# Gate and up stage of a streaming encoder step: row pieces handed out between products, nine row buffers, one preparation moved later

## The chip, the cores and the metric

The kernel runs on one core of a Trainium2 chip. The metric is the device time of one execution in microseconds (us). The core has five engines, each with its own instruction list that it works through in order: TensorE (PE, matmuls, with the weight loads shown as PEld), VectorE (DVE), ScalarE (ACT), GpSimd (POOL) and SyncE (SP, which here only issues DMA transfers). They wait for one another through semaphores.

## What is computed

One layer of a hybrid encoder runs on 2048 prompt rows and 128 sample rows of width 1024: a mixer of banded attention and convolution, a cross-attention into 256 memory tokens, and a dense SwiGLU network with 2816 hidden channels. The change lies in the first half of that network:

```python
D_MODEL = 1024; D_FF = 2816
h = rmsnorm(x, g_ffn_pre)
f = (jax.nn.silu(h @ w_gate) * (h @ w_up)) @ w_down
x = x + rmsnorm(f, g_ffn_post)
```

Everything is float32. The kernel splits each operand of a matmul into a rounded part ("hi", type fp32r) and the rest ("lo") and makes three matmuls of one product: hi by hi, hi by lo and lo by hi.

## The kernel before

The stages run one after the other: memory keys and values, projection, attention, mixer output, cross-attention (`phase_cross`), gate and up (`gate_up`), down. The change touches the end of `phase_cross` and the whole of `gate_up`.

**Cross-attention.** Sixteen tiles of 128 rows pass through scores, softmax (`z`), transposed probabilities (`probs`) and values. Behind some tiles stands `natural(g, p)`. It reads a pair of finished row tiles back (two DMA loads, L1304), norms each (ACT Square L1307, POOL L1309 and L1310, a DVE multiply L1311 over 1024 columns), makes four differences on POOL (L1312 to L1318) and stores seven combinations of the halves to the DRAM buffer `hn[g]` with four DMAs that POOL issues (L1313, L1315, L1317, L1319). There are nine such pairs, three for each of three row groups. A pair is taken as soon as its tiles are done and t is at least 4; the pair of tiles 12 and 14 was taken behind tile 15, and the last pair (13 and 15) in the first double block of `gate_up`.

**Gate and up.** The two matrix products are made with seven products of half size in place of eight (a Winograd-like scheme). For each of three row groups the seven forms of the rows are needed in transposed form: `tform(g, j)` makes one form in three *pieces*. A piece is a row load of 128 x 512 from `hn` (L1392, issued by SP into a buffer `nat`), four PE transposes into a PSUM buffer `tr` (L1395), the ACT copy of hi (L1397) and the DVE subtraction that gives lo (L1398). 21 pieces make a group ready. There were three `nat` buffers and there are two `tr` buffers. For each of 22 weight blocks, `wforms(f)` loads two weight tiles (L1404, L1405, into four buffers `wf`), makes the mixed forms on POOL (L1412 to L1415) and splits all seven (ACT L1417, DVE L1418). Nine buffer pairs `wh`, `wl` hold the split forms, so that two forms of the next block are ready ahead of a product. `product(ps, j, ...)` is 12 matmuls of 384 columns (three for each of four chunks; L283, L284 and L285 are the three matmuls of `mm3`), and a block has seven products. DVE and ACT combine the results (L1454 to L1482), and POOL makes the forms that the down stage reads (L1507 to L1510).

The first group's 21 pieces form *the opening* of the stage; the pieces for the next group are made during the last block of the group before (*the turn*), since each transposed form has one buffer only.

**What sets the order.** A scheduler takes the program's instructions and lays out each engine's list by a simulated clock, with priorities (`high_priority`) and with ties such as `issue_after(x)`, which keeps an instruction from being laid out ahead of x. So the lists differ from the order of the code, and they are fixed before the run. An engine that meets an instruction whose inputs aren't there waits, and all behind it wait too. That holds for SP as well: a row load that waits for its buffer holds up every weight load behind it.

## Time and profile before

| | us |
|---|---|
| median of 3 runs | 2948.85 (2946.77 to 2949.27) |
| the profiled execution | 2949.61 |
| its span in the profile | 2947.8 |
| PE busy | 2872.6 (97% of the span) |
| DVE busy | 2079.8 (71%) |
| POOL busy | 1371.4 (47%) |
| ACT busy | 1308.1 (44%) |

The table says that PE is busy nearly all the time, and that DVE, the next, has a quarter of its time free. These are means over stages that differ. The gate and up stage lies from about 1522 us to about 2490 us of the span; its opening runs from 1522 us to 1564 us, the first turn from about 1850 us to 1910 us, the second from about 2190 us to 2224 us.

### The profile page before, as it was taken

The page shows a single profiled execution, that of the slowest core. Times are in us where ns is not written, and L with a number is a line of the kernel's source. Part 1 is how long each engine was busy: PE and PEld are TensorE (multiplying, and loading weights), DVE is VectorE, ACT ScalarE, POOL GpSimd, SP SyncE. Part 2 cuts the span into 40 slices and gives each one's busy share as a digit, 9 for nine tenths or more (in the row PEclk, how much of TensorE's full clock was granted, in tenths as well). Part 3 has the DMA queues.
Part 4 walks back from the last instruction along what each step waited for, and adds up shares of the span by engine and source line. Part 5 has one row for each costly group of instructions (what it writes and reads, how often), then busy time and mean ns, then how long its engine had stood idle before and what let it go on. Part 6 is the DMA issues. An engine that isn't in the chain of part 4 may idle for free.

```text
span 2947.8 us, 45388 instructions
## 1 busy us (share of the span) xinstructions
PE 2872.6 (97%) x16740; PEld 2624.6 (89%) x16740; DVE 2079.8 (71%) x3024; ACT 1308.1 (44%) x2661; POOL 1371.4 (47%) x1247
## 2 busy tenths in 40 slices
PE   8999999979989999999999999999999999999998
PEld 8999999969978777888879999999999999888786
DVE  6697795969985336344469787788889997555655
ACT  4535364659874234232344333433344444333433
POOL 0268396730022224244557565465556775424413
PEclk9999999989999999999999999999999999999999
DMA  8735255558845665133355333644344446657754
GB/s 303 251 115 174 98 161 171 159 181 199 205 137 189 204 246 172 52 128 109 125 199 184 115 133 115 198 155 154 144 140 151 143 142 231 223 171 226 227 191 163
DMA packets 198474, 500.04 MB, mean 170 GB/s; under 512 B 18981, under 2 KB 87085, under 8 KB 189923
## 3 DMA queue, kind: packets, MB, share of 16 engines
q1 hardware_dynamic: 187931, 461.09, 48.4%
q0 software_dynamic: 10320, 36.05, 3.2%
q8 instruction: 131, 2.15, 0.3%
q14 instruction: 92, 0.75, 0.1%
HBM read 365.97 MB, written 141.81 MB: 172 GB/s over the span
## 4 chain that ended last, share of the span: by engine, by line
PE 43%; DMA 3%; POOL 2%; DVE 2%; issue 1%; ACT 0%; DVEq 0%; SPq 0%; POOLq 0%; ACTq 0%
PE psb L285 14%; PE psb L284 14%; PE psb L283 14%; PE psb L291 1%; DMA sbf<-in_w_down_dram 1%; DMA sbf<-x 1%; POOL sbf L1540 1%; PE psb L1395 1%; DMA sbf<-hn 1%; DVE sbr L1601 0%; POOL sbf L340 0%; DMA hn<-sbf 0%; DMA sbf<-in_w_gate_dram 0%; DVE flexb L1480 0%; DVE sbr L1418 0%
## 5 line engine op out<-in xcount | busy, mean ns | idle before, releaser
L283 PE MATMUL psb<-sbr 128*128 128x384 f32 (+3 forms) x2808 | 943.0, 337 | 3.7 <-ACT sbr L1600 1.5
L284 PE MATMUL psb<-sbr 128*128 128x384 f32 (+3 forms) x2356 | 806.1, 342 | 2.5 <-DVE sbr L320 2.4
L285 PE MATMUL psb<-sbr 128*128 128x512 f32 (+3 forms) x1848 | 633.9, 345 | 1.9 <-DVE sbr L1601 1.8
L283 PEld LDWEIGHTS psb<-sbr 128*128 128x128 f32 x2808 | 530.6, 189 | 33.6 <-ACT sbr L1600 2.6
L285 PE MATMUL psb<-sbr,sbx 128*128 128x384 f32 (+2 forms) x1484 | 476.7, 322 | 0.0
L284 PEld LDWEIGHTS psb<-sbr 128*128 128x128 f32 x2356 | 445.3, 189 | 29.5 <-DVE sbr L320 2.7
L285 PEld LDWEIGHTS psb<-sbr 128*128 128x128 f32 x1848 | 348.5, 189 | 31.4 <-DVE sbr L1601 4.6
L1418 DVE TENSOR_TENSOR sbr<-sbf,sbr 128x512 fp32r<-128x512 f32 x258 | 264.7, 1029 | 36.1 <-ACT sbr L1417 35.3
L1417 ACT CAST sbr<-sbf 128x512 fp32r<-128x512 f32 x258 | 159.4, 620 | 279.2 <-PE psb L284 231.4
L285 PEld LDWEIGHTS psb<-sbr,sbx 128*128 128x128 f32 x1484 | 280.5, 189 | 0.2
L523 DVE SCALAR_TENSOR_TENSOR psb<-sbf,psb 128x768 f32<-128x768 f32 (+1 forms) x290 | 264.2, 911 | 6.2
L291 PE MATMUL psb<-sbr 128*128 128x512 f32 x1004 | 247.3, 395 | 0.1
L1601 DVE TENSOR_TENSOR sbr<-sbf,sbr 128x384 fp32r<-128x384 f32 (+1 forms) x231 | 161.3, 721 | 94.3 <-ACT sbr L1600 93.4
L291 PEld LDWEIGHTS psb<-sbr 128*128 128x128 f32 x1004 | 185.8, 188 | 41.5 <-issue 2.5
L278 POOL TENSOR_TENSOR sbx<-sbf,sbr 128x1024 fp32r<-128x1024 f32 x60 | 152.9, 2550 | 81.2 <-ACT sbr L277 76.1
L1540 POOL TENSOR_TENSOR sbf<-sbf 128x512 f32<-128x512 f32 x77 | 106.2, 1385 | 169.2 <-DMA sbf<-in_w_down_dram 167.6
L1600 ACT CAST sbr<-sbf 128x384 fp32r<-128x384 f32 (+1 forms) x231 | 110.6, 497 | 165.2 <-PE psb L284 137.3
L533 POOL TENSOR_TENSOR flexb<-flexb,flexb 128x128 f32<-128x128 f32 (+1 forms) x180 | 167.4, 931 | 22.4 <-ACT flexb L532 12.9
L283 PE MATMUL psb<-sbr,sbx 128*128 128x384 f32 (+1 forms) x524 | 170.5, 327 | 1.2 <-ACT sbr L1397 0.7
L1417 ACT CAST sbx<-sbf 128x512 fp32r<-128x512 f32 x153 | 94.5, 620 | 160.9 <-PE psb L284 148.9
L291 PE MATMUL psb<-sbr,sbx 128*128 128x512 f32 x654 | 160.7, 397 | 4.1 <-ACT sbx L319 2.2
L1418 DVE TENSOR_TENSOR sbx<-sbf,sbx 128x512 fp32r<-128x512 f32 x153 | 152.4, 998 | 15.3 <-ACT sbx L1417 15.0
(328 smaller groups left out, 5938.8 us busy)
## 6 DMA issues: line engine op xcount, KB each, us to landing
af<-flexb SPq DMA_DIRECT2D x33, 1344.0 KB, 6.0
sbf<-in_w_down_dram SPq DMA_DIRECT2D x154, 256.0 KB, 3.7
sbf<-af SPq DMA_DIRECT2D x90, 384.0 KB, 4.2
sbf<-in_w_gate_dram SPq DMA_DIRECT2D x66, 512.0 KB, 3.3
sbf<-in_w_up_dram SPq DMA_DIRECT2D x66, 512.0 KB, 3.4
sbf<-x SPq DMA_DIRECT2D x50, 512.0 KB, 3.8
sbf<-in_w_in_dram SPq DMA_DIRECT2D x48, 512.0 KB, 3.9
sbr<-ks SPq DMA_DIRECT2D x28, 512.0 KB, 9.6
```

What stands on the lines that cost most here:

```text
L278: self.lo_engine.tensor_tensor(lo[:, :], wf[:, :], hi[:, :].bitcast(F32), ALU.subtract)
L283: nc.tensor.matmul(ps, lh, rh, start=start, stop=False, **kw)
L284: nc.tensor.matmul(ps, lh, rl, start=False, stop=False, **kw)
L285: self.last_product = nc.tensor.matmul(ps, ll, rh, start=False, stop=stop, **kw)
L291: self.last_half = nc.tensor.matmul(y[o], l, r[:, o * 512:(o + 1) * 512], start=start and x == 0, stop=stop and x == 2)
L523: nc.vector.scalar_tensor_tensor(acc if w < CW - 1 else o, src(w), cwt[:, j, w:w + 1], acc, ALU.mult, ALU.add)
L533: nc.gpsimd.tensor_tensor(o, o, v, ALU.add)
L1417: nc.scalar.copy(hs[j][:, :], src[j])
L1418: nc.vector.tensor_tensor(ls[j][:, :], src[j], hs[j][:, :].bitcast(F32), ALU.subtract)
L1540: nc.gpsimd.tensor_tensor(acc[:, :], acc[:, :], q[:, :], ALU.add if s > 0 else ALU.subtract)
L1600: nc.scalar.copy(ch[:, m], a[:, x, m])
L1601: nc.vector.tensor_tensor(cl[:, m], a[:, x, m], ch[:, m].bitcast(F32), ALU.subtract)
```

## The change

Four things change.

1. `nat` gets nine buffers in place of three: six more lie in the region that `natural` uses for its own tiles (offsets 0 to 12).
2. `tform` no longer does the work; it returns the two form tiles and a list of pieces. `next_rows(9)` keeps up to nine row loads out ahead, and `next_piece` does one piece. In `product`, a piece is done after every second chunk (six matmuls), and it is tied with `issue_after` to the last matmul emitted. In the turn the pieces so spread over the last block of a group and the following one.
3. The opening no longer makes whole forms; it takes the 21 pieces one after the other, with nine row loads ahead.
4. In `phase_cross` a pair is prepared only while t is below 15, so the pair of tiles 12 and 14 moves into `gate_up`, where `natural` is called in the first double block for it, and in the second for the pair of tiles 13 and 15.

No instruction is added or removed: each engine's list has as many instructions of each kind as before.

```diff
@@ phase_cross
-                if ready and t >= 4:
+                if ready and 4 <= t < NPT - 1:
@@ gate_up
-                .at("s", 2, (sbF, [26, 28, 38.5])).at("nat", 2, (sbF, [40.5, 42.5, 44.5]))
+                .at("s", 2, (sbF, [26, 28, 38.5])).at("nat", 2, (sbF, [40.5, 42.5, 44.5, 0, 2, 4, 6, 8, 10]))
...
         def tform(g, j):
             hi = self.t(pool, [P, 4, 3 * P], F32R, f"t{j}h")
             lo = self.t(pool, [P, 4, 3 * P], F32R, f"t{j}l")
-            for p in range(3):
+
+            def rows(p):
                 n = PAIRS[g][p][2]
                 x = self.t(pool, [P, 512], F32, "nat")
                 nc.sync.dma_start(x[:n, :], self.hn[g][:n, p, TFORM[j], :])
+                return x
+
+            def piece(p, x):
+                n = PAIRS[g][p][2]
                 ps = self.t(ps_tr, [P, 4, P], F32, "tr")
...
-            return hi, lo
+            return (hi, lo), [(lambda p=p: rows(p), lambda x, p=p: piece(p, x)) for p in range(3)]
+
+        raw, waiting = [], []
+
+        def next_rows(most):
+            while waiting and len(raw) < most:
+                first, second = waiting.pop(0)
+                raw.append((second, first()))
+
+        def next_piece(pin=False):
+            if not raw:
+                return
+            with ExitStack() as stack:
+                if pin:
+                    stack.enter_context(self.tc.issue_after(self.last_product.ins))
+                second, x = raw.pop(0)
+                second(x)
+            next_rows(9)
...
-        def product(ps, j, n, w, start):
+        def product(ps, j, n, w, start, turn=False):
...
+                if k % 2 and not (turn and j == 0):
+                    next_piece(True)
...
             for j in range(7):
-                ts[j] = tform(0, j)
+                ts[j], pieces = tform(0, j)
+                waiting += pieces
+            next_rows(9)
+            while raw:
+                next_piece()
...
-                    def after(j):
-                        if turn:
-                            nxt.append(tform(g + 1, j))
+                    if turn:
+                        for j in range(7):
+                            t, pieces = tform(g + 1, j)
+                            nxt.append(t)
+                            waiting.extend(pieces)
+                        next_rows(9)
...
-                    product(a, 0, n, w, True)
+                    product(a, 0, n, w, True, turn)
...
-                    after(0)
```

(The calls of `after(1)` to `after(6)` go too.) Some lines move by this: the transposes are L1395 before and L1400 after, the DVE subtraction of a piece L1398 and L1403, the row load L1392 and L1393, the weight loads L1404, L1405 and L1426, L1427, the DVE split of a weight form L1418 and L1440.

The first place is PE's list in the opening, at the twelfth and thirteenth pieces; `ident_73` is the identity matrix, `sbf` and `sbr` are the large SBUF tiles, `psb` is PSUM. Before:

```order
L285 MATMUL psb<-sbr 128x384
L1395 MATMUL psb<-ident_73,sbf 128x128 x8
L283 MATMUL psb<-sbr 128x384
L284 MATMUL psb<-sbr 128x384
L285 MATMUL psb<-sbr 128x384
```

And after:

```order
L285 MATMUL psb<-sbr 128x384
L1400 MATMUL psb<-ident_73,sbf 128x128 x8
L283 MATMUL psb<-sbr 128x384
L1400 MATMUL psb<-ident_73,sbf 128x128 x4
L284 MATMUL psb<-sbr 128x384
```

Pieces twelve and thirteen stand together in both (eight transposes); the fourteenth stood twelve matmuls behind them and now stands one matmul behind them.

The second place is DVE's list in the opening, from the last residual of the cross-attention (L339) on; L1311 is the multiply of `natural`, L1457 and L1462 combine products. Before:

```order
L339 SCALAR_TENSOR_TENSOR sbf<-psb,sbf 128x1024
L1398 TENSOR_TENSOR sbr<-psb,sbr 128x4x128
L1311 SCALAR_TENSOR_TENSOR sbf<-sbf,flexb_10314 128x1024
L1398 TENSOR_TENSOR sbr<-psb,sbr 128x4x128 x2
L1457 TENSOR_TENSOR sbf<-sbf,psb 128x384
L1398 TENSOR_TENSOR sbr<-psb,sbr 128x4x128 x2
L1311 SCALAR_TENSOR_TENSOR sbf<-sbf,flexb_10314 128x1024
L1398 TENSOR_TENSOR sbr<-psb,sbr 128x4x128
L1418 TENSOR_TENSOR sbr<-sbf,sbr 128x512
L1462 SCALAR_TENSOR_TENSOR flexb_12750<-flexb_12750,psb 128x384
L1398 TENSOR_TENSOR sbr<-psb,sbr 128x4x128 x2
```

And after:

```order
L339 SCALAR_TENSOR_TENSOR sbf<-psb,sbf 128x1024
L1403 TENSOR_TENSOR sbr<-psb,sbr 128x4x128 x3
L1486 TENSOR_TENSOR sbf<-sbf,psb 128x384
L1403 TENSOR_TENSOR sbr<-psb,sbr 128x4x128 x3
L1440 TENSOR_TENSOR sbr<-sbf,sbr 128x512
L1490 SCALAR_TENSOR_TENSOR flexb_12732<-flexb_12732,psb 128x384
L1403 TENSOR_TENSOR sbr<-psb,sbr 128x4x128 x2
```

The two multiplies of the moved pair are gone from between the pieces; they now stand around the seventeenth and eighteenth pieces, and those of the other pair, which stood around the twentieth, some twenty instructions behind the last piece.

The third place is SP's list around the same stretch; `hn_71_143` is the first group's row buffer in DRAM, and L1304 are the loads of `natural`. Before:

```order
L1304 DMA sbf<-x_12_66_138 128x1024
L1392 DMA sbf<-hn_71_143 128x512
L1404 DMA sbf<-in_w_gate_dram 128x1024
L1392 DMA sbf<-hn_71_143 128x512 x3
L1405 DMA sbf<-in_w_up_dram 128x1024
L1392 DMA sbf<-hn_71_143 128x512 x3
L1304 DMA sbf<-x_14_68_140 128x1024
L1392 DMA sbf<-hn_71_143 128x512 x4
L1405 DMA sbf<-in_w_up_dram 128x1024
L1392 DMA sbf<-hn_71_143 128x512 x5
L1404 DMA sbf<-in_w_gate_dram 128x1024
```

And after:

```order
L1393 DMA sbf<-hn_71_143 128x512
L1426 DMA sbf<-in_w_gate_dram 128x1024
L1427 DMA sbf<-in_w_up_dram 128x1024
L1393 DMA sbf<-hn_71_143 128x512 x6
L1426 DMA sbf<-in_w_gate_dram 128x1024
L1393 DMA sbf<-hn_71_143 128x512 x3
L1427 DMA sbf<-in_w_up_dram 128x1024
L1393 DMA sbf<-hn_71_143 128x512 x7
L1427 DMA sbf<-in_w_up_dram 128x1024
L1393 DMA sbf<-hn_71_143 128x512 x3
L1426 DMA sbf<-in_w_gate_dram 128x1024
```

The first row load now stands ahead of the first block's two weight loads (these stood ahead of all that is shown of before), and the loads of `natural` have left this stretch. The last up and gate loads shown are those of the second block, in both lists.

## Rows read from the trace of the kernel before

**Rows 1.** The profile page, its first line.
```profile
span 2947.8 us, 45388 instructions
```
**Rows 2.** Waits of PE, 1500 to 1600 us: engine, line, awaited; total us, times, longest.
```profile
PE psb L1395 <- DMA sbf<-hn: 1.8, 1, 1.8
PE psb L1395 <- DVE sbr L1398: 1.8, 3, 1.0
PE psb L283 <- DVE flexb L1468: 0.8, 1, 0.8
```
**Rows 3.** Waits of PE, 1600 to 2500 us.
```profile
PE psb L1395 <- DMA sbf<-hn: 3.0, 2, 1.9
PE psb L283 <- DVE flexb L1468: 1.0, 1, 1.0
```
**Rows 4.** Busy time of engines by stretch: stretch, length, PE, PEld, DVE, ACT, POOL, clock, DMA.
```profile
1521.98:1564.02 42.04, 36.94 (x217) 33.65 (x216) 35.11 (x41) 24.06 (x45) 30.95 (x30) 0.96 0.78 265
1564.02:1598.97 34.95, 34.11 (x197) 33.58 (x196) 33.91 (x41) 12.69 (x25) 28.42 (x22) 1.00 0.42 150
1600.00:1840.00 240.00, 240.00 (x1386) 240.00 (x1385) 194.60 (x267) 91.34 (x165) 138.40 (x99) 1.00 0.36 127
```
**Rows 5.** The same view, around PE's longest idle stretch of the opening.
```profile
1537.70:1541.10 3.40, 3.26 (x10) 2.83 (x10) 1.38 (x2) 0.59 (x1) 3.38 (x5) 0.53 0.81 206
```
**Rows 6.** PE's timeline in the opening: start, us, operation, count, idle before and releaser.
```profile
1521.98 0.34 PE L283 MATMUL psb<-sbr 128*128 128x384 f32 x1
...
1523.99 0.60 PE L1395 MATMUL psb<-ident,sbf 128*128 128x128 f32 x4
1524.34 0.42 PE L283 MATMUL psb<-sbr 128*128 128x384 f32 x1
1524.60 0.34 PE L284 MATMUL psb<-sbr 128*128 128x384 f32 x1
...
1536.43 1.33 PE L1395 MATMUL psb<-ident,sbf 128*128 128x128 f32 x8 [1.83 <-DMA sbf<-hn]
...
1564.02 0.42 PE L283 MATMUL psb<-flexb,sbx 128*128 128x384 f32 x1
```
**Rows 7.** DVE's timeline in the opening.
```profile
1524.47 1.28 DVE L339 SCALAR_TENSOR_TENSOR sbf<-psb,sbf 128x1024 f32<-128x1024 f32 x1
...
1526.26 3.03 DVE L1311 SCALAR_TENSOR_TENSOR sbf<-sbf,flexb 128x1024 f32<-128x1024 f32 x1
...
1532.46 2.36 DVE L1311 SCALAR_TENSOR_TENSOR sbf<-sbf,flexb 128x1024 f32<-128x1024 f32 x1
```
**Rows 8.** Pieces over the whole run: instances, shortest, median and longest in ns.
```profile
L1397 ACT CAST sbr<-psb x54: 364/586/623, 1510.4 to 2221.3; 128x512 fp32r<-128x512 f32 x48, 128x256 fp32r<-128x256 f32 x6
...
L1398 DVE TENSOR_TENSOR sbr<-psb,sbr x45: 407/680/692, 1511.0 to 2215.9; 128x512 fp32r<-128x512 f32 x40, 128x256 fp32r<-128x256 f32 x5
```
**Rows 9.** First and second block's weights: SP's, POOL's and ACT's timelines.
```profile
1478.28 0.33 SPq L1404 DMA_DIRECT2D sbf<-in_w_gate_dram  x1
...
1528.23 0.33 SPq L1405 DMA_DIRECT2D sbf<-in_w_up_dram  x1
...
1530.63 7.48 SPq L1392 DMA_DIRECT2D sbf<-hn  x5
...
1538.17 0.42 SPq L1404 DMA_DIRECT2D sbf<-in_w_gate_dram  x1
...
1532.46 1.29 POOL L1412 TENSOR_TENSOR sbf<-sbf 128x512 f32<-128x512 f32 x1 [1.13 <-DMA sbf<-in_w_up_dram]
...
1544.36 0.62 ACT L1417 CAST sbx<-sbf 128x512 fp32r<-128x512 f32 x1 [0.89 <-DMA sbf<-in_w_gate_dram]
```
**Rows 10.** DVE's groups by form, 1522 to 1600 us: count, busy us, mean ns, idle.
```profile
L1311 DVE SCALAR_TENSOR_TENSOR sbf<-sbf,flexb 128x1024 f32<-128x1024 f32 x4 | 8.0, 1990 | 0.6 <-POOL sbf L1310 0.5
```
**Rows 11.** `natural`'s multiply, 1400 to 1600 us, and the weight split, 1522 to 1600 us: shortest, median, longest.
```profile
L1311 DVE SCALAR_TENSOR_TENSOR sbf<-sbf,flexb x10: 1283/1285/3414, 1416.2 to 1562.0; 128x1024 f32<-128x1024 f32 x10
...
L1418 DVE TENSOR_TENSOR sbr<-sbf,sbr x15: 676/1306/1780, 1535.3 to 1593.2; 128x512 fp32r<-128x512 f32 x15
```

More of the change, by code (lines that the diff above doesn't have):

```diff
@@ L1452, in gate_up @@
                     tt, stt = nc.vector.tensor_tensor, nc.vector.scalar_tensor_tensor
-                    product(a, 0, n, w, True)
+                    product(a, 0, n, w, True, turn)
                     nc.scalar.copy(x1, a)
                     product(b, 1, n, w, True)
-                    after(0)
                     tt(x2, x1, b, ALU.add)
                     product(a, 2, n, w, False)
-                    after(1)
                     th = self.t(pool, [P, 3 * P], F32, "th")[:, :n]
@@ L1463, in gate_up @@
                     product(b, 3, n, w, False)
-                    after(2)
                     tt(x1, x1, b, ALU.add)
                     product(c, 4, n, w, True)
-                    after(3)
                     tt(x3, x1, c, ALU.add)
                     product(d, 5, n, w, True)
-                    after(4)
                     tt(x1, x1, d, ALU.subtract)
@@ L1474, in gate_up @@
                     product(c, 6, n, w, False)
-                    after(5)
-                    after(6)
                     tt(x2, x2, c, ALU.add)
```

## The prediction

> **What bounds the kernel now.** I read the page first: the span is 2947.8 us [rows 1], and PE is busy for nearly all of it, so only a shorter idle time of PE, or a faster clock, can shorten the run. The change leaves every engine's instructions as they are and only moves them. So the question is which idle times of PE lie in the gate and up stage, and who ends them. The waits of PE name them: in the opening 1.8 us for row loads and 1.8 us for DVE's subtraction L1398, one wait of 0.8 us for L1468 (a product's result being read out of PSUM) shortly after it [rows 2]; in all the rest of the stage 3.0 us in two waits for row loads, one in each turn, and 1.0 us for another L1468 [rows 3].
>
> Next the stretches [rows 4]. In the opening, 42.04 us, PE is busy 36.94 and DVE 35.11. In the 34.95 us behind it DVE is busy 33.91, that is 97%, although PE waits for it at the end of that stretch. In the steady part, 1600 to 1840, PE is never idle and DVE has 194.60 of 240, 81%. So PE bounds the steady part, but for the stretch from the opening to 1599 DVE works through a backlog, and the next thing that PE needs is late because DVE is.
>
> The clock: the granted clock is 0.53 between 1537.7 and 1541.1 [rows 5], about the lower of the two levels (1.2 of 2.4 GHz), and full on both sides. Just before it PE had stood idle 1.83 us for a row load [rows 6].
>
> **Part one: the opening as PE sees it.** A product costs 240.00/1386 = 0.173 us [rows 4]. A piece costs PE 0.35 us (its transposes start at 1523.99, the next product at 1524.34), and the product behind it takes 0.26 rather than 0.17 [rows 6]: 0.44 together. From 1521.98 to 1564.02 the list of before has 144 products and 18 pieces, 24.9 + 7.9 = 32.8 us. It took 42.04, so 9.2 us were lost, to waits and to the half clock. How much is lost in the new list?
>
> Nine row buffers put each row load nine pieces ahead; the wait of 1.83 us for rows goes. Three waits for `tr` stay or come, since there are still two `tr` buffers. The eighth piece needs the sixth's buffer, whose subtraction stands behind L339, which ends at 1524.47 + 1.28 = 1525.75 [rows 7]; with 0.68 for L1398 [rows 8] it is free at 1526.4. PE would be there at 1521.98 + 13 x 0.173 + 3 x 0.44 = 1525.5: 0.9 us. The eleventh piece stands one product behind the tenth and needs the ninth's buffer, which takes 0.35 + 0.59 + 0.68 [rows 8] plus hand-overs, some 1.8 us, against 0.9 of PE's own work: 0.9 us. The fourteenth now stands one product behind the thirteenth and needs the twelfth's buffer. In the new lists of ACT and DVE a weight split of the second block stands ahead of the twelfth piece. Its source comes from POOL's L1412, which started at 1532.46 when the up weights landed and took 1.29 [rows 9]. The up load stands behind the row loads of the eighth piece in both lists and so comes at about the same time. From 1533.75 the split on ACT (0.62), two more on ACT and on DVE, and L1398 end near 1536.3; PE is there at 1534.0: 2.4 us. With 0.5 us for the rest I have 4.7 lost in place of 9.2: PE by itself would gain 4.5 us, and the half clock goes with the wait that it followed.
>
> **Part two: the same stretch as DVE sees it.** This takes most of that back. Up to the readout that PE waited for at the end of the second stretch, DVE's two lists hold the same instructions, line by line: the moved multiplies L1311 of the first pair leave the opening's front, but all four are still ahead of that point. DVE was busy 35.11 + 33.91 = 69.0 of 76.99 us and idle 8.0. PE can pass that point earlier only by as much as DVE loses idle time. In the new list 1.9 us stay (no piece reaches DVE before 1523.9), and the gaps that I get from the walk above are 0.6 (eighth piece), 1.0 (first combined product), 0.6 (eleventh piece), 1.9 (POOL's L1412) and 0.7 (the gate weights): 6.7 us. So DVE, and with it PE, is 8.0 - 6.7 = 1.3 us earlier. The removal of the two L1311 (3.03 and 2.36 us [rows 7]) empties DVE where it then has nothing else to do, and fills it where it is late. I take **1.2 us gained** from 1522 to 1599. The bounds: 4.5 + 1.0 = 5.5 gained, if the splits get shorter and DVE keeps up; 4.4 lost (below, contention).
>
> The gate weights of the second block were issued at 1538.17 because SP stood 7.48 us at row loads, and ACT waited for them until 1544.36 [rows 9]. In the new list that load stands behind the row loads that follow the eleventh piece and can go out near 1532. This is part of PE's gain above, and it ends at the same backlog.
>
> The first row load now stands ahead of the first block's weights on SP. It waits until the softmax of tile 14 has been transposed, so these weights, loaded from 1478 on [rows 9], slip by some 9 us as I read it. Their block's products start at 1522 [rows 6], a good 30 us behind, and their splits are paced by POOL. I cost this at nothing; if the cover were gone, each us of lateness beyond it would cost one.
>
> **Part three: the turns.** With nine rows out ahead the two waits for row loads go: 3.0 us [rows 3]. DVE has time there (as in the steady part), so nothing takes their place at once. Bounds: 3.0 gained, or 1.0, if ACT's copy or the read-out of products is late next. I take **3.0 us gained**. The 1.0 us for L1468 behind the second turn stays.
>
> **Part four: what moves later.** `natural`'s stores now come later, and SP meets three row loads of the next group, which need the tiles that are stored, ahead of the seventh block's gate load. By POOL's list I take that load to go out 10 us or so later than before. A block's weights are loaded about two blocks ahead of its products, and a block is 84 x 0.173 = 14.5 us, so I cost nothing; beyond about 15 us each us would cost one. In the down stage the lists differ only in a few neighbours: nothing.
>
> **A rule that speaks against the change.** The row first: L1311 takes 1.28 us alone and up to 3.41 [rows 11], 1.99 on average for the four [rows 10], and the weight split takes from 0.68 to 1.78 [rows 11]; the piece's subtraction, whose source is PSUM, never goes above 0.69 [rows 8]. The Trainium skill, page "SBUF — State Buffer", section "Who interferes with whom", says that a DVE instruction with two SBUF inputs contends with a GpSimd instruction that reads SBUF, and that whoever comes second is blocked for the whole of the other. The trace agrees with it. By that rule the moved multiplies, now among POOL's weight forms, would all be long ones; that is a rival below, priced from rows.
>
> **The sum.** 1.2 + 3.0 = 4.2 us gained. The profiled execution took 2949.61 us, 0.76 above the median of 2948.85; its span of 2947.8 becomes 2943.6, the execution 2945.4, the median 2944.6. Within 0.2% (5.9 us) a measurement of this kernel can hardly tell from no change, so this counts as none.
>
> **Rivals.**
> *DVE keeps up.* If the backlog is not the limit, because DVE's splits are shorter when its work lies better against POOL's, PE gains its own 4.5, the 1.0 of the L1468 wait, and 3.0: 8.5 us, 2940.4. For it: split times range from 0.68 to 1.78. Against it: 97% busy in the second stretch.
> *All idle time goes.* The 9.2 of the opening, 1.0 and 3.0 with a part of the rest: 13.5 us, 2935.4. Against it: bunches of pieces still stand together in the new list.
> *Contention.* All four L1311 take the 3.41 us of the longest row: 13.6 in place of 8.0 [rows 10], 5.6 us more on DVE, so 4.4 lost in place of 1.2 gained; an idle PE of that length brings another stretch at half clock, 1.8 us (half of 3.4 us, as in rows 5); the turns give 3.0: 2948.85 + 4.4 + 1.8 - 3.0 = 2952.1. It decides as soon as the four average above about 2.3 us. Against it: in before, two of the four met POOL and two did not.
> *It doesn't do what it says.* The scheduler bunches pieces in the turns too, and a wait for DVE takes the place of that for rows: only 1.2 gained, 2947.6, no change.
>
> **How the numbers follow.** Forecast 0.50, contention 0.12, not what it says 0.08, DVE keeps up 0.25, all idle time 0.05. The last two are faster by over 0.2%, and so is a small part of the forecast's own spread (2941.5 to 2947.5): 0.33. Contention is over the bound in half its cases: 0.06. The rest, 0.61, is within it. The range 2938.5 to 2950.5 leaves out about 0.08 on each side.
>
> **What the profile of the changed kernel would show.** No wait of L1400 for row loads, in the opening or the turns; waits of L1400 for DVE of 1 to 2.5 us at the eighth, eleventh and fourteenth piece; the gate load of the second block near 1532; the end of the opening 3 to 5 us earlier but PE waiting for read-outs (L1494 or its neighbours) or for the last pieces between 1545 and 1600; full clock near 1538. The prediction is wrong if PE passes 1590 without a wait (then it is the faster case), if L1311 averages above 2.3 us, or if a row load is still waited for.

## The result: slower by 0.2%, and the profile after

The changed kernel takes 2956.57 us in the median of 14 runs (2952.35 to 2959.83), the kernel before 2948.65 beside it on the same chip; the ratio is 1.0021, with an interval from 1.0015 to 1.0028. A gain of 4.2 us was forecast; by the ratio the loss is about 6.2 us (0.0021 x 2949), by the medians 7.9. The profiled execution of after is its fastest, so the spans differ by less: 2950.6 us against 2947.8 [rows 1], 2.8 us.

```profile
span 2950.6 us, 45401 instructions
...
PE 2874.5 (97%) x16740; PEld 2628.2 (89%) x16740; DVE 2070.4 (70%) x3024; ACT 1309.3 (44%) x2661; POOL 1375.0 (47%) x1247
```

The waits of PE in the opening and shortly behind it (1500 to 1600 us), to be read beside [rows 2]; columns are the engine and line that waits, the awaited one, total us, times, longest:

```profile
PE psb L283 <- DVE sbf L1500: 4.2, 1, 4.2
PE psb L283 <- ACT sbr L1402: 2.8, 2, 2.5
PE psb L1400 <- DVE sbr L1403: 1.7, 4, 0.7
PE psb L283 <- ACT sbr L1439: 0.7, 1, 0.7
```

And in the rest of the stage (1600 to 2500 us), beside [rows 3]:

```profile
PE psb L283 <- DVE flexb L1494: 2.2, 1, 2.2
PE psb L285 <- DVE sbr L1624: 1.2, 1, 1.2
PE psb L283 <- DVE sbf L1500: 0.5, 1, 0.5
```

No wait for a row load is left anywhere: 1.8 and 3.0 us are gone. In their place stands one wait of 4.2 us for L1500, the read-out of a product, that before does not have.

The busy time by stretch (length, PE, PEld, DVE, ACT, POOL, clock, DMA), beside [rows 4, 5]:

```profile
1521.10:1563.00 41.90, 36.78 (x227) 34.20 (x226) 33.35 (x42) 22.07 (x41) 26.04 (x22) 1.00 0.60 188
1563.00:1598.60 35.60, 30.06 (x169) 28.84 (x167) 29.70 (x34) 11.51 (x22) 29.80 (x28) 0.97 0.56 208
1596.80:1603.50 6.70, 4.82 (x15) 4.82 (x16) 6.70 (x9) 2.96 (x6) 4.42 (x4) 0.50 0.66 208
```

The opening itself has PE busy at full clock. In the stretch behind it DVE is busy 29.70 of 35.60 us, not 97% as before, while POOL rises from 28.42 of 34.95 to 29.80 of 35.60 (81 to 84%). And the lower of the two clock levels, 0.50, is granted around and behind PE's long idle time.

I compared the start of each matmul with the start of the matmul of the same number in the trace of before (PE's lists have 16740 each). The difference is -0.9 us where the opening begins, -4.4 at 1537 us, -2.6 at 1582, then +4.9 at 1601; it falls to +1.8 in the first turn, is +2.6 behind it, ends the second at +1.8, rises to +3.8 behind it (L1494) and to +5.1 at the start of the down stage (L1624), and ends at +2.9. So the opening gains 3.5 and gives 1.8 of it back, one place loses 7.5, the turns gain some 3, and 3.3 are lost behind them. From the start of the opening to the start of the down stage that is 6.0 us lost, about the ratio's 6.2. In the down stage, where the lists differ only in a few neighbours, 2.3 come back; there the other traces lie between 0.8 lost and 2.5 gained, so I don't count this for the change.

That place, in the four engines' timelines (start, us, engine, line, operation, tiles, count, idle before and releaser). PE first, with the wait in the opening that stands where the forecast had one:

```profile
1535.93 0.44 PE L283 MATMUL psb<-sbr 128*128 128x384 f32 x1 [2.54 <-ACT sbr L1402]
...
1594.00 0.45 PE L283 MATMUL psb<-sbr 128*128 128x384 f32 x1 [0.69 <-ACT sbr L1439]
...
1598.68 0.69 PE L283 MATMUL psb<-sbr 128*128 128x384 f32 x1 [4.24 <-DVE sbf L1500]
```

DVE of after, the same time:

```profile
1590.31 0.54 DVE L1490 SCALAR_TENSOR_TENSOR flexb<-flexb,psb 128x384 f32<-128x384 f32 x1
1593.46 4.70 DVE L1440 TENSOR_TENSOR sbr<-sbf,sbr 128x512 fp32r<-128x512 f32 x1 [2.61 <-ACT sbr L1439]
1598.09 0.54 DVE L1500 TENSOR_TENSOR sbf<-sbf,psb 128x384 f32<-128x384 f32 x1
```

ACT, which makes the first half of each split:

```profile
1587.06 0.62 ACT L1439 CAST sbx<-sbf 128x512 fp32r<-128x512 f32 x1 [5.38 <-POOL sbf L1434]
...
1592.81 1.14 ACT L1439 CAST sbr<-sbf 128x512 fp32r<-128x512 f32 x2 [4.74 <-POOL sbf L1436]
```

And POOL:

```profile
1583.68 1.65 POOL L1312 TENSOR_TENSOR sbf<-sbf 128x512 f32<-128x512 f32 x1 [0.84 <-DVE sbf L1311]
1585.30 1.73 POOL L1434 TENSOR_TENSOR sbf<-sbf 128x512 f32<-128x512 f32 x1
1586.99 1.28 POOL L1314 TENSOR_TENSOR sbf<-sbf 128x512 f32<-128x512 f32 x1
1588.24 1.60 POOL L1316 TENSOR_TENSOR sbf<-sbf 128x512 f32<-128x512 f32 x1
1589.80 1.74 POOL L1435 TENSOR_TENSOR sbf<-sbf 128x512 f32<-128x512 f32 x1
1591.49 1.29 POOL L1436 TENSOR_TENSOR sbf<-sbf 128x512 f32<-128x512 f32 x1
1592.72 0.57 POOL L1315 DMA_DIRECT2D hn<-sbf  x1
1593.31 1.28 POOL L1318 TENSOR_TENSOR sbf<-sbf 128x512 f32<-128x512 f32 x1
1594.53 0.57 POOL L1317 DMA_DIRECT2D hn<-sbf  x1
1595.12 1.27 POOL L1437 TENSOR_TENSOR sbf<-sbf 128x512 f32<-128x512 f32 x1
1596.35 1.26 POOL L1434 TENSOR_TENSOR sbf<-sbf 128x512 f32<-128x512 f32 x1
1597.55 0.57 POOL L1319 DMA_DIRECT2D hn<-sbf  x1
```

Read it from the bottom. POOL does the four differences of the second moved pair (L1312, L1314, L1316, L1318) and its stores in between the four weight forms of one block (L1434 to L1437): these take from 1585.30 to 1596.39, 11.1 us. ACT waits for them 5.38 and 4.74 us, DVE waits 2.61 for ACT. Then DVE's split L1440, which takes 0.68 us alone, takes 4.70: from just behind the store L1315 to 1598.16, which is 0.55 us behind the end of POOL's last subtraction, L1434 at 1597.61. L1500 stands behind the split in DVE's order, and PE waits for that.

### The profile page after: what moved, and what is told of

Read it like the earlier page. It is cut to its first block, busy times and chain, and to the rows that moved or that the text cites. A ratio compares the mean times of both kernels' runs of the same rounds, so it can differ in the third digit from the quotient of the medians.

```text
span 2950.6 us, 45401 instructions
## 1 busy us (share of the span) xinstructions
PE 2874.5 (97%) x16740; PEld 2628.2 (89%) x16740; DVE 2070.4 (70%) x3024; ACT 1309.3 (44%) x2661; POOL 1375.0 (47%) x1247
## 5 line engine op out<-in xcount | busy, mean ns | idle before, releaser
L1440 DVE TENSOR_TENSOR sbr<-sbf,sbr 128x512 fp32r<-128x512 f32 x258 | 254.8, 989 | 39.8 <-ACT sbr L1439 38.2
L1624 DVE TENSOR_TENSOR sbr<-sbf,sbr 128x384 fp32r<-128x384 f32 (+1 forms) x231 | 164.4, 733 | 103.1 <-ACT sbr L1623 101.3
L1440 DVE TENSOR_TENSOR sbx<-sbf,sbx 128x512 fp32r<-128x512 f32 x153 | 148.8, 975 | 15.6 <-ACT sbx L1439 15.0
```

The lines of the kernel that those rows point to most:

```text
L1440: nc.vector.tensor_tensor(ls[j][:, :], src[j], hs[j][:, :].bitcast(F32), ALU.subtract)
L1624: nc.vector.tensor_tensor(cl[:, m], a[:, x, m], ch[:, m].bitcast(F32), ALU.subtract)
```

## The experiments

Each ratio is to the kernel before on the same chip, from 5 rounds; without other words an edit is to the kernel after. The half-widths of the intervals are 0.0008 to 0.0014, or 2.5 to 4 us. Where a run's trace is compared with that of before, it is by the start of the matmul of the same number, as above, and there is one trace of each.

**Where the pairs stand.** First the moved line by itself, undone in after and done alone in before.

```diff
-                if ready and 4 <= t < NPT - 1:
+                if ready and t >= 4:
```

> The changed kernel with one line undone: the pair of tiles 12 and 14 is prepared behind tile 15 again, the rest stays (nine row buffers, pieces handed out between products). POOL theory (the loss comes from the second pair's differences on POOL, which stand among the weight forms of the fifth and sixth block and make a split, and by it a read-out of PSUM, late): in this kernel POOL's list has the second pair where the kernel before had it, so no read-out is waited for by more than 1.5 us near 1590, no half clock there, and the time is 2947 to 2951. DVE theory (PE comes out of the opening earlier than DVE can follow, wherever the pairs stand): the opening is still fed by nine buffers, so PE waits 3 us or more for a read-out between 1564 and 1610, and the time is 2953 to 2957. Under both the row loads beyond the third must wait for the pair's tiles, so five pieces stand in one bunch and the opening loses some us to that.

Measured 2977.24 us, 1.0097 [1.0083, 1.0110], far above both theories' figures, so the run decides nothing between them. The row loads wait for the pair, since the six added row buffers lie on the tiles of its preparation. Its waits of PE, 1500 to 1600 us:

```profile
PE psb L1400 <- DMA sbf<-hn: 14.4, 2, 14.1
```

So nine buffers in the opening force the pair out of it. The line alone, in before:

> The kernel before with one line changed: the pair of tiles 12 and 14 is prepared in the gate and up stage; three row buffers and whole forms as before. If the moved line by itself costs the time: 2954 to 2957. If it costs only together with the nine buffers, which lie on the pair's own tiles and keep it back (POOL theory: POOL's list here has both pairs where the kernel before had them): 2947 to 2950, with the row waits of before (near 1.8 us in the opening, 3.0 in the turns) and no read-out waited for by over 1.5 us near 1590. DVE theory: also 2947 to 2950, since PE isn't early here.

Measured 2949.86, 1.0002 [0.9994, 1.0011]: the scheduler put the pairs at the same places of POOL's list as in before, but for some exchanged neighbours. Next, the second pair, and then both, still later among the weight blocks, where DVE has slack (81% busy, [rows 4]):

```diff
-                    if g == 0 and x == 1 and self.todo:
+                    if g == 0 and x == 1 and fp == 0:
                         self.natural(*self.todo.pop(0))
+                    if g == 0 and x == 1 and fp == 4:
+                        with self.tc.issue_after(self.last_load.ins):
+                            self.natural(*self.todo.pop(0))
```

> The changed kernel with the second pair (tiles 13 and 15) tied behind the weight loads of the eleventh block, so that its loads, multiplies and differences fall some 60 us later, where DVE is four fifths busy. POOL theory: the wait of 4.2 us for a read-out near 1594 and the half clock behind it (7 us together in the profile) go, the opening's 3.5 and the first turn's 2.3 us stay gained: 2943 to 2947. DVE theory: only the two multiplies' 3.3 us leave the stretch, a read-out is still waited for by 1 to 3 us near 1590, and the clock may fall again: 2949 to 2954. If the loss lies somewhere else altogether (turns, down stage): 2955 to 2958.

Measured 2958.74, 1.0033 [1.0021, 1.0046], above every figure expected; PE waits 5.9 us for L1494 at the pair's new place. With both pairs late (`fp in (4, 6)`):

> The changed kernel with both pairs tied behind weight loads (of the eleventh and the fifteenth block). POOL theory: as with the second pair alone, perhaps 1 us less, since the first pair's differences no longer stand among the third block's weight forms: 2942 to 2947. DVE theory: all four multiplies (6.5 us) leave the stretch, so PE can come out of it up to 3 us earlier than in the kernel before: 2944 to 2948, and clearly faster than with the second pair alone. If the loss lies elsewhere: 2955 to 2958.

Measured 2963.96, 1.0051 [1.0039, 1.0064], again above every figure. The stall near 1598 is gone in both runs, and stands where the pair now is; in the run with both pairs late, 1670 to 1750 us:

```profile
PE psb L283 <- DVE sbf L1486: 7.2, 1, 7.2
PE psb L283 <- DVE flexb L1494: 5.2, 1, 5.2
```

Each of these waits is followed by some 6.8 us at half clock. The stall goes with the pair. It is no floor of DVE's behind the opening.

**What in the pair costs.** In both late runs a DVE instruction again took 5.8, 6.4 and 7.9 us while POOL worked on without a break. Theory A says that DVE is shut out there by POOL's stores with tensor work between them; theory B that POOL has too much to do, so that the forms come late; theory C, added later, that the pair loads POOL, ACT and DVE at once and relief of one does not do. Three edits take away one candidate each. The stores of the two late pairs go from POOL to SP; the first of the four, and the call:

```diff
-            nc.gpsimd.dma_start(dst[:n, p, 0:2, :], xa)
+            store(dst[:n, p, 0:2, :], xa)
...
-                        self.natural(*self.todo.pop(0))
+                        self.natural(*self.todo.pop(0), store=nc.sync.dma_start)
```

> The kernel after, with the four stores of each of the last two pairs' prepared rows issued by SyncE instead of GpSimd (the differences stay on GpSimd). In the kernel after, PE waits 4.24 us at 1598.7 behind a VectorE weight split that took 4.70 us instead of 0.68, while GpSimd ran weight forms between its stores L1315, L1317 and L1319. Theory A (the split is shut out of the memory port that it shares with GpSimd, from one store to the next, when tensor work stands between the stores): without stores on GpSimd no VectorE instruction there is over 2.5 us, the wait falls under 1.5 us, the half clock behind it goes, and the time is near 2949 (4.2 + 3.4 less than 2956.6). Theory B (GpSimd has too much work there, so the forms come late whatever the stores do): only four issues of 0.6 us go, the wait stays over 2.5 us and the time is 2954 or more. SyncE now waits for the differences, so a late row or weight load may show under either; then the length of the VectorE splits is what decides.

Measured 2952.99 (before there 2951.06), 1.0008 [0.9999, 1.0017]: between A's figure and B's, with waits of 1.8, 1.5 and 1.2 us left. Next, the four differences of these two pairs go from POOL to DVE (`nc.gpsimd.tensor_tensor` to `nc.vector.tensor_tensor` in L1312 to L1318):

> The kernel after, with the four differences of each of the last two pairs on VectorE instead of GpSimd (some 0.7 us each there); the stores stay on GpSimd, and in its list two weight forms now stand between the second pair's stores L1315 and L1317. Theory A (shut out between stores): a VectorE instruction with two operands in SBUF still takes over 2.5 us there, and PE still waits 2 us or more near 1595; 2954 to 2958. Theory B (too much work on GpSimd): GpSimd has 5.8 us less per pair, the forms come in time, the wait falls under 1 us; 2949 to 2951. The theory of the prediction (VectorE full) would have the wait grow by 2.8 us: 2959 or more.

Measured 2956.80, 1.0020 [1.0011, 1.0030]; a DVE instruction of 3.41 us, from just behind the start of the store L1315 to the end of L1317, and a wait of 3.6 us. The time is in A's range, but the run is no clean trial of B: with the differences DVE has work without a break, 22.64 of the 22.70 us from 1580.3 to 1603.0. Next, the last three stores in a row, behind the block's last form:

```diff
-            nc.gpsimd.dma_start(dst[:n, p, 6, :], xa[:, 1, :])
...
+            with ExitStack() as stack:
+                if self.last_form is not None:
+                    stack.enter_context(self.tc.issue_after(self.last_form.ins))
+                nc.gpsimd.dma_start(dst[:n, p, 4:6, :], tt)
+                nc.gpsimd.dma_start(dst[:n, p, 2:4, :], xb)
+                self.last_store = nc.gpsimd.dma_start(dst[:n, p, 6, :], xa[:, 1, :])
...
+            with ExitStack() as stack:
+                if f and self.last_store is not None:
+                    stack.enter_context(self.tc.issue_after(self.last_store.ins))
+                tt(src[4], u[:, 0, :], u[:, 1, :], ALU.add)
...
```

> The kernel after, with the last three stores of a pair tied behind its last difference and behind the weight block's last form, and the next block's forms tied behind the last store: the same instructions on GpSimd among the same blocks, but the three stores stand in a row with no tensor instruction between them. Theory A: no VectorE instruction over 2.5 us there, the wait at 1594 to 1599 falls from 4.2 to under 1.5, no half clock near 1600; 2948 to 2951. Theory B: as the kernel after or worse, since the forms stand no earlier; 2955 to 2958.

Measured 2954.47, 1.0011 [1.0002, 1.0020], between the two theories' figures. In this run and in the one with the stores on SP no DVE instruction of the stretch is over 2.1 us, as theory A said. But with the stores together PE still waits, for the next product's read-out. DVE of that run, then PE:

```profile
1595.58 1.18 DVE L1512 SCALAR_TENSOR_TENSOR flexb<-flexb,sbf 128x384 f32<-128x384 f32 x1
1596.68 3.41 DVE L1447 TENSOR_TENSOR sbx<-sbf,sbx 128x512 fp32r<-128x512 f32 x2
1600.02 0.54 DVE L1501 TENSOR_TENSOR flexb<-sbf,psb 128x384 f32<-128x384 f32 x1
...
1600.61 0.44 PE L283 MATMUL psb<-flexb,sbr 128*128 128x384 f32 x1 [3.72 <-DVE flexb L1501]
```

Two splits at 1.7 us each have taken the place of one at 4.70. So the one long instruction is not the bound, and theory A falls as the whole cause. Theory B is not settled by these runs: the one that takes the differences from POOL fills DVE instead. So I priced the second pair as a whole: its rows loaded and stored (by SP), nothing computed of them; and then only its differences left out, with its stores on SP (`leave` is 2 for the pair, 1 for the differences).

```diff
+                if leave == 2:
+                    continue
...
+            if leave:
+                nc.sync.dma_start(dst[:n, p, 0:2, :], xa)
...
+                return
```

> The kernel after, with the second of the two late pairs left out: its rows are still loaded, but nothing is computed of them and SyncE stores them as they came, so the output is not the reference's. It prices the moved pair as a whole. If the 4.24 us wait at 1598.7 and the 3.4 us of half clock behind it are the pair's, both go, no wait of PE over 1.5 us stands between 1570 and 1610, and the time is 2956.6 - 7.6 = 2949, 2947 to 2950. If they come from PE reaching that place earlier and not from the pair (the theory of the prediction, a floor under the second half of the opening), a wait of 2.5 us or more stays there and the time is 2954 or more.

Measured 2949.46 (before there 2949.31), 1.0004 [0.9995, 1.0013]. No wait of PE stands between 1570 and 1610. POOL's forms of the same block, which took 11.1 us, take from 1581.51 to 1587.47, 6.0 us:

```profile
1581.51 1.30 POOL L1442 TENSOR_TENSOR sbf<-sbf 128x512 f32<-128x512 f32 x1 [1.23 <-DMA hn<-sbf]
1582.89 1.77 POOL L1443 TENSOR_TENSOR sbf<-sbf 128x512 f32<-128x512 f32 x1
1584.61 1.29 POOL L1444 TENSOR_TENSOR sbf<-sbf 128x512 f32<-128x512 f32 x1
1585.86 1.61 POOL L1445 TENSOR_TENSOR sbf<-sbf 128x512 f32<-128x512 f32 x1
```

> The kernel after, with only the four differences of the second late pair left out and its four stores on SyncE (output not the reference's): ScalarE's sums of squares, GpSimd's four small instructions and VectorE's two scalings L1311 stay. It takes 5.8 us of differences and 2.3 us of stores from GpSimd. Theory B (the weight forms come late because GpSimd does the pair's differences between them): as with the whole pair left out, within 1.5 us: 2948 to 2951. Theory C (the pair loads three engines that have little to spare, and relief of one is not enough): a wait of 2 us or more stays between 1570 and 1610 and the time is 2951.5 to 2955.

Measured 2952.95, 1.0013 [1.0004, 1.0021]. The time is in theory C's range; of the two waits left at 1570 to 1610 none is the 2 us that C named:

```profile
PE psb L283 <- DVE flexb L1502: 1.1, 1, 1.1
PE psb L283 <- DVE flexb L1498: 1.0, 1, 1.0
```

The pair costs 0.0017, some 5.0 us; by the ratios about half goes with differences and stores, about half with the sums of squares on ACT, the scalings L1311 on DVE and four small instructions on POOL. The halves are no finer than the intervals. The traces divide it otherwise: from 1570 to 1605 us after loses 7.4 us on before, the run without differences and stores 1.6, and that without the pair gains 1.1. So 5.9 of 8.5 us go with differences and stores there.

**The pair spread.** The loads and scalings first, then one difference and its store behind each of the next four blocks' forms; all the work is done.

```diff
...
+                    if g == 0 and f > 0:
+                        if not self.staged and self.todo:
+                            self.staged = [self.stages(*self.todo.pop(0))]
+                        for stage in self.staged:
+                            with self.tc.issue_after(self.last_form.ins):
+                                if next(stage, 0) == 0:
+                                    self.staged = []
```

> The kernel after, with the work of each of the two late pairs spread over five weight blocks: first the loads, sums and scalings, then one difference and its store behind the forms of each of the next four blocks. All work is done. Theory B: no block's forms wait for more than one difference (1.3 to 1.7 us), so no wait of PE over 1.5 us at the pairs; 2948 to 2951. Theory C: waits of 1 to 2 us remain at the blocks with the scalings, 2950 to 2953. If the pair costs what it costs wherever and however it is done: 2955 or more.

Measured 2950.35, 1.0007 [0.9999, 1.0016]: two waits, 1.7 us together, between 1570 and 1640, no stall. The time lies in B's range and in C's.

**Opening and turns apart.** Three buffers (`nat0`) for the first group, nine for the turns, pairs where before has them, pieces spread:

```diff
-                x = self.t(pool, [P, 512], F32, "nat")
+                x = self.t(pool, [P, 512], F32, "nat" if g else "nat0")
...
```

> The kernel after, with three row buffers for the first group's pieces (their own 3 tiles, as before) and nine for the two turns only, and with the pairs allowed behind the last tile again; the pieces stay one per six matmuls. GpSimd's list then has the pairs where the kernel before has them (its stores L1315, L1317, L1319 with one difference between the first two and no weight form). Both theories: no VectorE instruction over 3 us at 1560 to 1600, the turns' row waits (3.0 us) stay away. What differs from before is then the opening's list and the turns: 2944 to 2947, 2 to 4 us under the kernel before. If the gain of the turns is given back in any case, 2948 to 2949.

Measured 2951.85 (before 2951.06), 1.0000 [0.9991, 1.0008]: too low a time was expected; by 1570 us the spread opening on three buffers loses 2.2 us to before (4.4 us of waits for the pieces' subtraction), by 1605 1.1, and from there to 2495 1.2 more: these turns, with nine buffers and spread pieces, gain nothing. Nine for the turns alone, in the kernel before:

> The kernel before, with nine row buffers for the two turns only: pieces, pairs and the opening's three buffers stay. PE waited 3.0 us for row loads at the turns; these go. If that is a gain, 2945.5 to 2947.5. If the next wait takes it (VectorE's read-out, 1.0 us before and 2.2 us after at 2255), 2948 to 2949.5.

Measured 2947.84 (before 2949.31), 0.9994 [0.9985, 1.0002]. The trace gains 2.9 us at the first turn and 1.3 around the second, and gives 1.3 back at the start of the down stage (L1602 is L1624 of after); that much cannot be told from no change. The turns' pieces of after put back where before has them, three behind each product:

```diff
-                if k % 2 and not (turn and j == 0):
+                if k % 2 and not turn:
                     next_piece(True)
...
-                    product(b, 1, n, w, True)
+                    product(b, 1, n, w, True, turn)
+                    after(0)
...
```

> The kernel after, with the pieces of the two turns put where the kernel before has them (three behind each product, not tied, no longer one per six matmuls); nine buffers, the opening and the late pairs stay as after. In the kernel after the second turn gives back 2 us at 2258 (PE waits 2.2 us for VectorE's read-out L1494, against 1.0 before). If the spread is what costs there, that wait falls under 1.2 us and the time is 2 us under after: 2954 to 2955.5. If the nine buffers cost it (the pieces all come early and VectorE's own work piles up behind them), the wait stays at 2 us or more and the time is that of after, 2956 to 2957.5.

Measured 2952.69 (before 2948.18), 1.0017 [1.0008, 1.0026]. The wait of 2.2 us behind the second turn falls to 0.2; the 4.3 at the pair stands. So the spread, not the nine buffers, cost these 2 us in the trace; in the medians of these two runs they are within the interval. All the traces say the same: from 1605 us (or from where the late pairs are done) to 2495, the eleven with spread pieces lose 0.0 to 2.0 us on before, the four with nine buffers and before's pieces gain 2.7 to 3.6. (The kernel with the moved line alone, on three buffers, gains 1.6 there, so a part of this may be chance of the one trace of before.) The 1.2 us at the start of the down stage is gone here too, but the run with nine buffers for the turns alone had 1.4 there with pieces that are not spread; what decides it was not tried. Both cures together:

> The late pairs spread over five weight blocks each, as in the run that spread them, and the turns' pieces where the kernel before has them, with nine buffers everywhere. If the two gains add (5 us from the spread pair, 2 us from the turn): 2956.6 - 7 = 2949.5 on a chip where before takes 2948.7, less if the opening's 3.5 us then stay: 2946 to 2949. If the opening gives its gain back in any case: 2949 to 2951.

Measured 2944.69, 0.9988 [0.9979, 0.9997], lower than expected. It differs from the run with the pair spread (1.0007 [0.9999, 1.0016]) in the turns alone, so there the medians show the spread pieces' cost too. And the spread pair with three buffers and before's pieces in the opening:

> The kernel before, with nine row buffers for the two turns only, and the last two pairs behind the opening, spread over five weight blocks each. It asks whether the opening gains by the pair's absence alone, without nine buffers and without spread pieces: the pair's two scalings (3.03 and 2.36 us on VectorE) and its rows' loads leave the opening. If it does: 2 to 4 us under the kernel before with nine buffers at the turns, so 2944 to 2946. If the opening is bound by its 21 pieces on three buffers: the same 2947 to 2949 as with nine at the turns alone, or above that by the 1 to 2 us that the spread pair still costs.

Measured 2943.15 (before 2948.18), 0.9981 [0.9972, 0.9990]: the fastest of all, though with the row wait still in its opening (waits of PE, 1500 to 1600 us):

```profile
PE psb L1406 <- DMA sbf<-hn: 2.5, 1, 2.5
PE psb L1406 <- DVE sbr L1409: 1.1, 3, 0.5
```

Between 1600 and 2500 its longest wait is 0.9 us. From 1525 to 1601 it gains 1.8 us on before, the two runs with the pair spread and with nine buffers and spread pieces in the opening 2.1 and 1.4; by 1650, with the spread pairs' waits, 1.0, 0.5 and 0.1 are left. So the opening gains a little by the pair's absence, and the turns by nine buffers with before's pieces; nine buffers and spread pieces in the opening add nothing that shows. A gain clear of no change came out only in the two runs that have both: the pair moved and spread, and such turns.

## Why the prediction was wrong, point by point

**The failed step is part four**, "what moves later", which costed the moved pair at nothing. Measured, it is 5.0 us. The step looked only at SP's gate load, and never counted the moved step's own instructions on POOL: four differences and three stores, 7.5 us in the rows above, and 10.1 with the first store and the small ones just ahead of them, between forms that a block needs every 14.5 us. In the steady part POOL is busy 138.40 of 240 us [rows 4], some 8.4 of each 14.5, so as an estimate the pair and a block's own work come to 18.5, more than there is. The prediction's part on a rule that speaks against the change came near, and then asked only whether the four L1311 would be long. In the sum, the 1.2 us gained up to 1599 became 5.7 lost; the 3.0 of the turns, the second term, became 0.2 lost.

**Part one held in the main.** PE gained 3.5 us by 1537 but 1.8 by the end of the opening, where 4.5 were forecast; no wait for rows is left, the second block's gate load goes out at 1533.83 (1532 forecast), and the profiled run has full clock near 1538. The wait of 2.4 us at the fourteenth piece came as 2.54, but as one place: a product that waits for ACT's copy of the piece (L1402), behind a weight split. The full clock there was luck: eight of the ten variants above that keep this opening show a stretch at half clock behind that wait.

**Part two, the floor of DVE, was wrong in its reason.** It held that DVE, 97% busy, must pass L1468 by only 1.2 us earlier. It counted DVE's idle time over both stretches down from 8.0 us to 6.7. In after the same 81 instructions are:

```profile
1521.10:1603.50 82.40, 71.66 (x409) 67.86 (x408) 67.96 (x81) 36.54 (x69) 58.94 (x51) 0.96 0.58 196
```

Busy 67.96 us, 1.1 less than before in spite of the long split, and idle 14.4. So DVE was not the floor: it waited, most of all for ACT's copies and splits. Of 4.7 us behind the opening, 2.61 are the wait shown above and 2.08 one for a split that stands in ACT's list behind the pair's first sum of squares, L1307, which waited for its rows:

```profile
1573.75 1.06 ACT L1307 ACTIVATE sbf<-sbf 128x1024 bf16<-128x1024 f32 x1 [2.85 <-DMA sbf<-x]
1574.81 0.60 ACT L1439 CAST sbr<-sbf 128x512 fp32r<-128x512 f32 x1
1575.44 1.38 DVE L1440 TENSOR_TENSOR sbr<-sbf,sbr 128x512 fp32r<-128x512 f32 x1 [2.08 <-ACT sbr L1439]
```

(With the pair left out PE gained 2.9 us from 1525 to 1601, but two L1311 leave DVE with it, so that run alone would not refute a floor of DVE's.) "Busy" included the time that DVE's instructions stood blocked by POOL: 8.0 us for four L1311, for example, that take 1.28 alone [rows 10, 11]. In after they are shorter, not longer:

```profile
L1311 DVE SCALAR_TENSOR_TENSOR sbf<-sbf,flexb 128x1024 f32<-128x1024 f32 x4 | 6.5, 1627 | 0.4 <-POOL sbf L1310 0.4
```

**Part three** was right on the waits for rows, 3.0 us, and wrong that nothing takes their place: between 1605 and 2495 us the trace loses 0.2 where 3.0 gained were forecast. The turns gain some 3, but the read-out L1468 behind the second turn (L1494 in after) grows from 1.0 to 2.2 us, and 1.2 come at L1624. With nine buffers and before's pieces the turns' 2.7 stay in the trace, as the run with nine for the turns shows; by the traces it is the spread pieces that take them.

**The rivals.** *Contention* came nearest in time (2952.1), in part by luck, since it counted 3.0 gained at the turns. It named blocked instructions of DVE, but the wrong one: its point of decision, L1311 above 2.3 us, was not met (1.63). The blocked one was the weight split L1440, 4.70 us against 1.78 at the longest in before [rows 11]. *DVE keeps up* and *all idle time goes* fell. *It doesn't do what it says* had the turns right, where a wait for DVE takes the place of that for rows, but not the loss. The sign that the prediction named, a wait for a read-out between 1545 and 1600, came; it was 4.24 us long.

**What stays open.** The spans differ by 2.8 us and the medians by 6 to 8; the trace's own loss in this stage is 6.0, and what the other executions lose has no trace. How the pair's 5.0 us divide between late forms (DVE idle 2.61 us), the rest of its instructions and blocked DVE instructions is not settled: the runs with the stores moved (1.0008 and 1.0011) and that with the differences left out (1.0013) lie within each other's intervals. In the traces, from 1570 to 1605, the runs with the stores on SP lose 5.0 us, with the stores in a row 7.1 and with the differences on DVE 7.8; two kernels with the pair at the same place (after, and the one with the turns as before) lose 7.4 and 8.4, so a microsecond says little there.

## What to carry to other kernels

A step that is moved carries its instructions to every engine's queue: add up their time on each engine, and set it against the time that engine has left beside what it must deliver for every block at the new place. If one engine feeds another that feeds a third (POOL, ACT, DVE, PE here), spread such a step over several blocks rather than find a better place for the whole. A share of busy time that includes blocked instructions is no floor.

## What the runs showed of the hardware

By the timing of the traces, a DVE instruction with two inputs in SBUF can stand blocked for several POOL instructions in a row, not for one alone. From 1530 us on, at the pairs' places, eleven splits, combinations and differences in ten runs took 3.0 to 7.9 us. Each began 0.2 to 0.9 us after POOL had begun one of the pair's stores, with tensor work on POOL behind that store; with the stores on SP, or in a row, none is over 2.1 us. It does not happen behind each store: in before a combination L1480 that began 0.5 us behind L1315 took 1.78. During the longest POOL's forms took 1.26 to 1.30 us, against 1.6 to 1.75 where the two engines seem to take turns. The Trainium skill, page "SBUF — State Buffer", section "Who interferes with whom", calls the port pair that the two share an exclusive lock and says that issue order decides who blocks. The trace agrees that DVE blocks and shows more, a wait over seven POOL instructions:

```profile
1739.82 7.89 DVE L1440 TENSOR_TENSOR sbr<-sbf,sbr 128x512 fp32r<-128x512 f32 x1
```

```profile
1739.40 0.57 POOL L1317 DMA_DIRECT2D hn<-sbf  x1
1740.00 1.30 POOL L1435 TENSOR_TENSOR sbf<-sbf 128x512 f32<-128x512 f32 x1
...
1746.16 0.99 POOL L1534 TENSOR_TENSOR flexb<-flexb 128x384 f32<-128x384 f32 x1
```

That is the run with both pairs late: the split began 0.42 us behind L1317 and ends at 1747.71, 0.56 us behind the end of L1534, POOL's seventh instruction behind that store. Why stores between the tensor instructions go with it is not shown.
